# Macaron hybrid layer: another order and other engines for the opening stage's modulation sums and weight splits

## The chip, the cores and the metric

The kernel runs on one core of one Trainium2 chip. The metric is the device time of one execution in microseconds. Engines are named as the profile names them: PE is TensorE (its weight loads are PEld), DVE is VectorE, ACT is ScalarE, POOL is GpSimd, SP is SyncE, which issues the DMAs here. `L89` is line 89 of the kernel before.

## What is computed

One layer over 512 tokens of width 1024: modulation from a condition vector, a gated feed-forward, a mixer (chunked mLSTM and forgetting attention), and a second feed-forward. The change touches the beginning alone:

```python
mod = silu(c) @ w_ada + b_ada                       # c: 1 x 1024, w_ada: 1024 x 9216
sh1, sc1, g1, ... = split(mod, 9)
u = rms_norm(x, ffn1_norm_g) * (1 + sc1) + sh1      # 512 x 1024
a, b = split(u @ ffn1_w_in, 2)                      # ffn1_w_in: 1024 x 5632
x = x + 0.5 * g1 * ((silu(a) * b) @ ffn1_w_out)
```

## The kernel before

Every float32 matmul is made of three in a rounded format: each operand is split into a high part and a remainder, and `uh*wh`, `uh*wl` and `ul*wh` are added up in PSUM. For weights, `split` (L81) makes the high part `wh` on ACT (L88) and the remainder `wl` by a subtraction (L89), on DVE unless another engine is given.

The opening stage is `start` (L397). `x` is loaded and normalised, and then the first 3 of the 22 column pairs of `ffn1_w_in` are multiplied (six PSUM banks, `NJ0` = 3) while the modulation is still being made. A *block* is 128 of the 1024 channels of `u`. For each of the eight blocks k the stage does this:

- `mod(k)` (L432): the shift and scale of the block's 128 channels need `silu(c)` times 1024 x 128 columns of `w_ada`, twice. Four DMAs bring them as eight pieces of 128x256; DVE makes two running sums that take turns (`acc[i % 2]`): two products (L442), six multiply-adds, called *links* here (L444), and an addition of the two (L445). Block 0 is summed on PE instead (`mod0`, L423).
- `load(k)` (L449): the block's feed-forward weights, 128x768, into `raw`, of which there are three buffers.
- `prep(k)` (L452): two one-column matmuls add the sum up over the partitions (L454); two small steps make shift and scale from it (on DVE, L458 and L459; for block 0 on ACT, L461 and L462); four transposes on PE bring the block's `x` (L422); `split` makes `wh` and, on POOL, `wl`; `u_from` (L239) makes `uh` and `uf` on ACT and their difference `ul` (L248), on POOL for block 0, on DVE for the others.
- 18 matmuls on PE (L490). The first three blocks take all six `uh*wh` first, then the six `uh*wl`, then the six `ul*wh`; the others go bank by bank. `prep(k + 1)` is issued behind the seventh.

The order on each engine comes from a scheduler in the framework, by the program's order and a cost estimate; `issue_after` puts an instruction behind another one on the same engine. Each engine runs its instructions in order, and SP issues its DMAs in order too, so that a load that waits for a free buffer holds up those behind it.

Behind the stage `ffn_in` (L333) goes on with the other 19 column pairs, with weights split by `w_stat` (L92), and `ada_row` (L273) makes further rows of the modulation on DVE from 128x1024 loads.

Of the kernel before, what the change touches and what calls it, by code (L numbers as in the profile page):

```python
# [46 lines left out]
class Layer:  # L47
    def __init__(self, tc, es, A, out, dbg=None):
        self.tc, self.nc, self.es, self.A, self.out = tc, tc.nc, es, A, out
        self.dbg = dbg or {}  # L50
# [188 lines left out]
    def u_from(self, ps, k, c0, w, G, sh, pool, start=False):  # L239
# [8 lines left out]
        (nc.gpsimd if (k == 0 if start else k % 2) else nc.vector).tensor_tensor(  # L248
# [148 lines left out]
    def start(self, st, tp):  # L397
# [25 lines left out]
        def mod0():  # L423

            for v in range(2):
                r = st.tile([P, NK, P], F32, name=self.nm("ar"), tag="ar", bufs=15)
                nc.sync.dma_start(r, A["w_ada"][0][:, v * D:v * D + P].rearrange("(i p) n -> p i n", p=P))
                turn(0, (v,))
                turn(1, (v,))
                for i in range(NK):  # L430
                    nc.tensor.matmul(cb[:, 128 * (v + 1):128 * (v + 2)], r[:, i, :], self.ccol[:, i:i + 1].to_broadcast([P, P]), start=i == 0, stop=i == NK - 1)
        def mod(k):  # L432
            acc = [st.tile([P, 2, P], F32, name=self.nm("ac"), tag="ac", bufs=6) for _ in range(2)]
            for q in range(2):
                r = st.tile([P, 4, 2, P], F32, name=self.nm("ar"), tag="ar", bufs=15)
                for v in range(2):
                    nc.sync.dma_start(r[:, :, v, :], A["w_ada"][0][q * 512:(q + 1) * 512, v * D + k * P:v * D + (k + 1) * P]
                                      .rearrange("(i p) n -> p i n", p=P))
                for i in range(4):
                    a, cc = acc[i % 2], self.ccol[:, 4 * q + i:4 * q + i + 1]  # L440
                    if q == 0 and i < 2:
                        nc.vector.tensor_scalar(a, r[:, i], cc, None, op0=MUL)  # L442
                    else:
                        nc.vector.scalar_tensor_tensor(a, r[:, i], cc, a, op0=MUL, op1=ADD)  # L444
# [7 lines left out]
        def prep(k):  # L452
# [3 lines left out]
            wr = raws.pop(k)  # L456
            if k:
                nc.vector.tensor_tensor(m[:, 0:1], cb[:, 2 * k:2 * k + 1], self.colC[:, 16 + k:17 + k], op=ADD)  # L458
                nc.vector.tensor_scalar(m[:, 1:2], cb[:, 2 * k + 1:2 * k + 2], self.colC[:, 8 + k:9 + k], self.colC[:, 24 + k:25 + k], op0=MUL, op1=ADD)  # L459
            else:  # L460
                nc.scalar.activation(m[:, 0:1], cb[:, 128:129], AF.Identity, bias=self.colC[:, 16:17])  # L461
                nc.scalar.activation(m[:, 1:2], cb[:, 256:257], AF.Identity, scale=self.colC[:, 8:9], bias=self.colC[:, 24:25])  # L462
# [612 lines left out]
```

## Time and profile before

| what | us |
|---|---|
| median of three runs | 1375.53 (1375.0 to 1376.16) |
| the profiled execution's own time | 1374.87 |
| its span in the trace | 1372.9 |
| PE busy in the span | 1344.6 |
| DVE busy | 800.8 |
| ACT busy | 554.1 |
| POOL busy | 130.5 |

The trace is that of one execution. Its times count from the span's start. A matmul's duration in the trace overlaps the next one's, so the rate is read from the distance of their starts. Where an engine idles, the row of the timeline names what ended the wait; for a wait on several things that is the last of them as far as the profile can tell, and where the engine named had long been done it was another, often a DMA.

### The profile page before, as it was taken

The numbers are of one execution on the slowest core, as the hardware profiler recorded it, in microseconds if no ns is written. First come the engines' busy times: TensorE is split into PE (matmuls) and PEld (weight loads), VectorE is DVE, ScalarE is ACT, GpSimd is POOL, SyncE is SP. The second block draws the span as 40 slices with busy tenths as digits, with TensorE's granted clock in tenths as the row PEclk, the third lists the DMA queues.
The fourth block names the chain that finished last, engine by engine and source line by source line (L and its number), as shares of the span: only waits on it lengthen the run. The fifth ranks groups of instructions, "written<-read, shape, count | busy, mean of one in ns | idle before, by whom it ended". The sixth has DMA issues, their size and how long they took to land.

```text
span 1372.9 us, 17542 instructions
## 1 busy us (share of the span) xinstructions
PE 1344.6 (98%) x6570; PEld 1126.7 (82%) x6570; DVE 800.8 (58%) x1440; ACT 554.1 (40%) x939; POOL 130.5 (10%) x151
## 2 busy tenths in 40 slices
PE   6999999999999999999999999899999999999998
PEld 5788887887888888888888878788898888888887
DVE  7865666656467776876585876456473333332232
ACT  4442333323237655556565675333262322322120
POOL 4200000000011100313130311002010000000000
PEclk9999999999999999999999999999999999999999
DMA  9766556665534434344343342364323333333330
GB/s 288 206 203 182 181 182 203 210 214 187 184 82 111 121 96 139 118 112 132 88 140 85 112 139 77 117 198 138 107 71 114 92 95 105 92 93 104 102 123 31
DMA packets 217001, 184.42 MB, mean 134 GB/s; under 512 B 10898, under 2 KB 182578, under 8 KB 216916
## 3 DMA queue, kind: packets, MB, share of 16 engines
q1 hardware_dynamic: 216436, 183.22, 44.2%
q8 instruction: 52, 0.85, 0.2%
q14 instruction: 33, 0.27, 0.1%
q0 software_dynamic: 416, 0.06, 0.0%
q10 hardware_dynamic: 64, 0.02, 0.0%
HBM read 172.71 MB, written 10.56 MB: 133 GB/s over the span
## 4 chain that ended last, share of the span: by engine, by line
PE 87%; DVE 7%; ACT 2%; issue 1%; SPq 1%; DMA 1%; POOL 0%; ACTq 0%; DVEq 0%; POOLq 0%
PE g L108 23%; PE g L106 23%; PE g L107 23%; PE t L106 4%; PE t L107 4%; PE t L108 4%; PE t L820 2%; DVE wl L89 1%; PE t L790 1%; PE t L761 1%; PE t L762 1%; DMA ar<-in_w_ada_dram 1%; DVE ac L444 1%; SPq L78 1%; ACT wh L88 1%
## 5 line engine op out<-in xcount | busy, mean ns | idle before, releaser
L89 DVE TENSOR_TENSOR wl<-raw,wh 128x1024 fp32r<-128x1024 f32 x214 | 276.1, 1292 | 277.7 <-ACT wh L88 254.2
L88 ACT ACTIVATE wh<-raw 128x1024 fp32r<-128x1024 f32 (+1 forms) x221 | 231.6, 1053 | 503.4 <-PE g L107 160.3
L108 PE MATMUL g<-uh,wl 128*128 128x512 f32 (+2 forms) x984 | 369.6, 376 | 1.8 <-DVE wl L89 1.8
L106 PE MATMUL g<-uh,wh 128*128 128x512 f32 (+2 forms) x984 | 370.6, 377 | 0.0
L107 PE MATMUL g<-ul,wh 128*128 128x512 f32 (+2 forms) x984 | 369.7, 376 | 0.0
L108 PEld LDWEIGHTS g<-uh,wl 128*128 128x128 f32 (+1 forms) x984 | 184.6, 188 | 36.3 <-DVE wl L89 2.7
L106 PEld LDWEIGHTS g<-uh,wh 128*128 128x128 f32 (+1 forms) x984 | 184.8, 188 | 34.0 <-issue 0.6
L107 PEld LDWEIGHTS g<-ul,wh 128*128 128x128 f32 (+1 forms) x984 | 184.8, 188 | 33.3
L106 PE MATMUL g<-wh,uh 128*128 128x512 f32 (+1 forms) x320 | 111.8, 350 | 0.0
L108 PE MATMUL g<-wh,ul 128*128 128x512 f32 (+1 forms) x320 | 111.1, 347 | 0.0
L107 PE MATMUL g<-wl,uh 128*128 128x512 f32 (+1 forms) x320 | 111.0, 347 | 0.0
L325 DVE TENSOR_TENSOR sl<-g,sl 128x512 f32<-128x512 f32 (+1 forms) x45 | 30.0, 667 | 85.7 <-PE g L108 85.5
L284 DVE SCALAR_TENSOR_TENSOR acc<-raw,ccol,acc 128x1024 f32<-128x1024 f32 x49 | 62.9, 1283 | 15.7 <-DMA raw<-in_w_ada_dram 15.2
L106 PE MATMUL g<-wh,hh 128*128 128x512 f32 x176 | 69.2, 393 | 0.0
L108 PE MATMUL g<-wh,hl 128*128 128x512 f32 x176 | 69.1, 393 | 0.0
L106 PE MATMUL t<-wh,hh 128*128 128x512 f32 x176 | 69.0, 392 | 0.0
L107 PE MATMUL g<-wl,hh 128*128 128x512 f32 x176 | 69.0, 392 | 0.0
L107 PE MATMUL t<-wl,hh 128*128 128x512 f32 x176 | 69.0, 392 | 0.0
L108 PE MATMUL t<-wh,hl 128*128 128x512 f32 x176 | 69.0, 392 | 0.0
L106 PEld LDWEIGHTS g<-wh,uh 128*128 128x128 f32 x320 | 60.5, 189 | 7.8 <-DVE tk L674 0.5
L108 PEld LDWEIGHTS g<-wh,ul 128*128 128x128 f32 x320 | 60.5, 189 | 7.8
L107 PEld LDWEIGHTS g<-wl,uh 128*128 128x128 f32 x320 | 60.5, 189 | 7.4
(264 smaller groups left out, 1921.6 us busy)
## 6 DMA issues: line engine op xcount, KB each, us to landing
raw<-in_ffn_w_in_dram SPq DMA_DIRECT2D x82, 512.0 KB, 3.8
raw<-in_w_ada_dram SPq DMA_DIRECT2D x56, 512.0 KB, 3.4
raw<-in_w_mix_dram SPq DMA_DIRECT2D x48, 512.0 KB, 4.0
raw<-in_ffn_w_out_dram SPq DMA_DIRECT2D x44, 512.0 KB, 3.9
raw<-in_w_mix_dram SPq DMA_DIRECT2D x32, 256.0 KB, 3.0
ar<-in_w_ada_dram SPq DMA_DIRECT2D x28, 256.0 KB, 6.0
g_d<-tg SPq DMA_DIRECT2D x16, 256.0 KB, 3.3
A<-A_d SPq DMA_DIRECT2D x16, 256.0 KB, 3.5
```

Source lines behind the costliest of these rows:

```text
L78: self.nc.sync.dma_start(dst(t), src)
L88: nc.scalar.activation(hi, src, AF.Copy)
L89: (eng or nc.vector).tensor_tensor(lo, src, hi, op=SUB)
L106: mm(ps, lh, rh, start=start, stop=False)
L107: mm(ps, lh, rl, start=False, stop=False)
L108: self.last_mm = mm(ps, ll, rh, start=False, stop=stop)
L284: nc.vector.scalar_tensor_tensor(acc, r, self.ccol[:, k:k + 1], acc, op0=MUL, op1=ADD)
L325: nc.vector.tensor_tensor(s[:, :w], ps_b[:, c0:c1], s[:, :w], op=MUL)
L444: nc.vector.scalar_tensor_tensor(a, r[:, i], cc, a, op0=MUL, op1=ADD)
L761: nc.tensor.matmul(ps[:, :w], q[:, s], k[:, :w], start=True, stop=False)
L762: nc.tensor.matmul(ps[:, :w], q[:, s], kl[:, :w], start=False, stop=True)
L820: nc.tensor.matmul(po[:, q0:], vt[pr][:, kb, i % 2, :], Px[:, o:o + T - q0], start=n == 1, stop=n == 8)
```

## The change

In the opening stage:

- The sum of a block is one chain on DVE: one product and seven links, each on the result of the one before. Blocks 2 and 3, and blocks 4 and 5, are summed in pairs, so that one chain handles 128x512 pieces for two blocks. The loads are cut to match (rows of 1 KB for pairs).
- `wl` is made on DVE for blocks 1 to 7 and on POOL for block 0 alone; block 0's `ul` moves from POOL to DVE.
- Shift and scale are made on ACT for every block.
- `split` for block k + 1 is traced ahead of `prep(k + 1)`, and `mod(k + 2)` behind the former `ul` and `wl`. Loads have their own buffers, eight for `w_ada`, and go ahead of the sums: `fetch`.
- Behind the stage, the first splits and the first product of `ada_row` are put behind the last `uf` and `ul`.

```diff
@@ split
-            nc.scalar.activation(hi, src, AF.Copy)
-        (eng or nc.vector).tensor_tensor(lo, src, hi, op=SUB)
+            with self.tc.issue_after(self.last_uf.ins) if self.lo_after else nullcontext():
+                nc.scalar.activation(hi, src, AF.Copy)
+        with self.tc.issue_after(self.lo_after) if self.lo_after else nullcontext():
+            self.last_lo = (eng or nc.vector).tensor_tensor(lo, src, hi, op=SUB)
@@ u_from
-        (nc.gpsimd if (k == 0 if start else k % 2) else nc.vector).tensor_tensor(
+        self.last_ul = (nc.gpsimd if not start and k % 2 else nc.vector).tensor_tensor(
@@ ada_row
-                nc.vector.tensor_scalar(acc, r, self.ccol[:, 0:1], None, op0=MUL)
+                with self.tc.issue_after(self.last_ul.ins):
+                    nc.vector.tensor_scalar(acc, r, self.ccol[:, 0:1], None, op0=MUL)
@@ start
+        def ada_load(k, n):
+            w = n * P
+            rows = 8 // n
+            ars[k] = []
+            for q in range(n):
+                r = new_ar().rearrange("p (i v c) -> p i v c", v=2, c=w)
+                step = 4 if k == 0 else rows
+                for v in range(2):
+                    for i0 in range(0, rows, step):
+                        r0 = (q * rows + i0) * P
+                        nc.sync.dma_start(r[:, i0:i0 + step, v, :], w_ada[r0:r0 + step * P, v * D + k * P:v * D + k * P + w]
+                                          .rearrange("(i p) n -> p i n", p=P))
+                ars[k].append(r)
...
         def mod(k):
-            acc = [st.tile([P, 2, P], F32, name=self.nm("ac"), tag="ac", bufs=6) for _ in range(2)]
...
-            nc.vector.tensor_tensor(acc[0], acc[0], acc[1], op=ADD)
-            accs[k] = acc[0]
+            tiles = ars.pop(k)
+            n = len(tiles)
+            acc = st.tile([P, 2, n * P], F32, name=self.nm("ac"), tag=f"ac{n}", bufs=4 - n)
+            for i in range(NK):
+                r, cc = tiles[i * n // NK][:, i % (NK // n)], self.ccol[:, i:i + 1]
+                if i:
+                    nc.vector.scalar_tensor_tensor(acc, r, cc, acc, op0=MUL, op1=ADD)
+                else:
+                    nc.vector.tensor_scalar(acc, r, cc, None, op0=MUL)
+            for j in range(n):
+                accs[k + j] = acc[:, :, j * P:(j + 1) * P]
@@ prep
-                nc.vector.tensor_tensor(m[:, 0:1], cb[:, 2 * k:2 * k + 1], self.colC[:, 16 + k:17 + k], op=ADD)
...
+            nc.scalar.activation(m[:, 0:1], c[0], AF.Identity, bias=self.colC[:, 16 + k:17 + k])
+            nc.scalar.activation(m[:, 1:2], c[1], AF.Identity, scale=self.colC[:, 8 + k:9 + k], bias=self.colC[:, 24 + k:25 + k])
...
-                wh, wl = self.split(wr, sh, nc.gpsimd)
+        groups = {0: 1, 1: 1, 2: 2, 4: 2, 6: 1, 7: 1}
+        def fetch(k):
+            ada_load(k, groups[k])
+            for j in range(groups[k]):
+                load(k + j)
@@ loop over the blocks
                 if n == 6 and k + 1 < NK:
+                    ul_ins = self.last_ul.ins
+                    with self.tc.issue_after(self.last_uf.ins):
+                        w = self.split(raws.pop(k + 1), sh)
+                    lo_ins = self.last_lo.ins
                     with self.tc.issue_after(self.last_uf.ins), self.tc.issue_after(mm.ins):
-                        nxt = prep(k + 1)
+                        prep(k + 1)
+                    nxt = w
+                    if k + 2 == NK - 1:
+                        ul_ins = self.last_ul.ins
+                    if k + 2 in groups:
+                        with self.tc.issue_after(ul_ins), self.tc.issue_after(lo_ins):
+                            mod(k + 2)
```

The names below are the program's with running numbers: `ac` a running sum, `ar` its w_ada piece, `raw`, `wh` and `wl` a block's weights, `g_190` to `t_195` the six PSUM banks, `uh_174` and `ul_182` block 0's, the next numbers the next blocks'.

PE in block 0, before: behind the six `uh*wh` and the first `uh*wl` come the one-column matmuls for block 1 (L454) and two transposes.

```order
L490 MATMUL t_195<-uh_174,wh_327 128x512
L490 MATMUL g_190<-uh_174,wl_328 128x512
L454 MATMUL t_196<-one,ac_298 128x1 x2
L422 MATMUL t_273<-ident,xn_237 128x128
L422 MATMUL t_273<-ident,xn_241 128x128
L490 MATMUL g_191<-uh_174,wl_328 128x512
L490 MATMUL g_192<-uh_174,wl_328 128x512
L490 MATMUL g_193<-uh_174,wl_328 128x512
L490 MATMUL t_194<-uh_174,wl_328 128x512
L490 MATMUL t_195<-uh_174,wl_328 128x512
L490 MATMUL g_190<-ul_182,wh_327 128x512
L490 MATMUL g_191<-ul_182,wh_327 128x512
```

The same place now:

```order
L428 MATMUL t_279<-ident,xn_241 128x128
L504 MATMUL g_191<-uh_174,wl_324 128x512
L504 MATMUL g_192<-uh_174,wl_324 128x512
L504 MATMUL g_193<-uh_174,wl_324 128x512
L504 MATMUL t_194<-uh_174,wl_324 128x512
L504 MATMUL t_195<-uh_174,wl_324 128x512
L504 MATMUL g_190<-ul_182,wh_323 128x512
L470 MATMUL t_196<-one,ac_305 128x1 x2
L504 MATMUL g_191<-ul_182,wh_323 128x512
L504 MATMUL g_192<-ul_182,wh_323 128x512
L504 MATMUL g_193<-ul_182,wh_323 128x512
L504 MATMUL t_194<-ul_182,wh_323 128x512
```

The one-column matmuls (L470) stand behind all six `uh*wl` and the first `ul*wh`; five matmuls of block 0 follow them, where eleven did.

DVE from block 1's `ul` on, before: the sum of block 3 (`ac_384`, `ac_385`), with shift and scale of block 2 (L458, L459) and its `ul` in between.

```order
L445 TENSOR_TENSOR ac_331<-ac_331,ac_332 128x256
L442 TENSOR_SCALAR ac_384<-ar_386,ccol 128x256
L442 TENSOR_SCALAR ac_385<-ar_386,ccol 128x256
L444 SCALAR_TENSOR_TENSOR ac_384<-ar_386,ccol,ac_384 128x256
L444 SCALAR_TENSOR_TENSOR ac_385<-ar_386,ccol,ac_385 128x256
L458 TENSOR_TENSOR m_413<-t_196,colC 128x1
L459 TENSOR_SCALAR m_413<-t_196,colC 128x1
L444 SCALAR_TENSOR_TENSOR ac_384<-ar_393,ccol,ac_384 128x256
L444 SCALAR_TENSOR_TENSOR ac_385<-ar_393,ccol,ac_385 128x256
L444 SCALAR_TENSOR_TENSOR ac_384<-ar_393,ccol,ac_384 128x256
L444 SCALAR_TENSOR_TENSOR ac_385<-ar_393,ccol,ac_385 128x256
L248 TENSOR_TENSOR ul_184<-uf_425,uh_176 128x512
```

The same place now, from block 1's remainder on:

```order
L92 TENSOR_TENSOR wl_359<-raw_302,wh_358 128x768
L459 SCALAR_TENSOR_TENSOR ac_305<-ar_299,ccol,ac_305 128x256
L461 TENSOR_SCALAR ac_373<-ar_327,ccol 128x512
L459 SCALAR_TENSOR_TENSOR ac_373<-ar_327,ccol,ac_373 128x512 x3
L251 TENSOR_TENSOR ul_183<-uf_369,uh_175 128x512
L459 SCALAR_TENSOR_TENSOR ac_373<-ar_330,ccol,ac_373 128x512 x2
L92 TENSOR_TENSOR wl_401<-raw_333,wh_400 128x768
L459 SCALAR_TENSOR_TENSOR ac_373<-ar_330,ccol,ac_373 128x512 x2
L251 TENSOR_TENSOR ul_184<-uf_414,uh_176 128x512
```

Two remainders (`wl_359` of block 1, `wl_401` of block 2) stand among the links; `ac_373` is the one chain for blocks 2 and 3, and block 2's `ul` follows it.

DVE at the end of the stage, before: the last links of block 7's sum and block 6's shift and scale, and the next stage's first remainders (L89) ahead of block 7's `ul`.

```order
L444 SCALAR_TENSOR_TENSOR ac_609<-ar_617,ccol,ac_609 128x256
L444 SCALAR_TENSOR_TENSOR ac_608<-ar_617,ccol,ac_608 128x256
L444 SCALAR_TENSOR_TENSOR ac_609<-ar_617,ccol,ac_609 128x256
L458 TENSOR_TENSOR m_637<-t_196,colC 128x1
L459 TENSOR_SCALAR m_637<-t_196,colC 128x1
L445 TENSOR_TENSOR ac_608<-ac_608,ac_609 128x256
L248 TENSOR_TENSOR ul_188<-uf_649,uh_180 128x512
L458 TENSOR_TENSOR m_673<-t_196,colC 128x1
L459 TENSOR_SCALAR m_673<-t_196,colC 128x1
L89 TENSOR_TENSOR wl_790<-raw_787,wh_789 128x1024
L89 TENSOR_TENSOR wl_820<-raw_817,wh_819 128x1024
L248 TENSOR_TENSOR ul_189<-uf_685,uh_181 128x512
```

The same place now:

```order
L251 TENSOR_TENSOR ul_188<-uf_588,uh_180 128x512
L461 TENSOR_SCALAR ac_592<-ar_480,ccol 128x256
L92 TENSOR_TENSOR wl_620<-raw_483,wh_619 128x768
L459 SCALAR_TENSOR_TENSOR ac_592<-ar_480,ccol,ac_592 128x256 x7
L192 COPY colA<-t_666 128x112
L251 TENSOR_TENSOR ul_189<-uf_633,uh_181 128x512
L286 TENSOR_SCALAR acc_800<-raw_802,ccol 128x1024
L92 TENSOR_TENSOR wl_738<-raw_735,wh_737 128x1024
```

All of block 7's sum (`ac_592`) stands behind block 6's `ul`, its links behind block 7's remainder as well; the next stage's first product (`acc_800`) and remainder stand behind block 7's `ul`.

## Rows read from the trace of the kernel before

**Rows 1.** The page: span; busy time, share and instructions of each engine.
```profile
span 1372.9 us, 17542 instructions
PE 1344.6 (98%) x6570; PEld 1126.7 (82%) x6570; DVE 800.8 (58%) x1440; ACT 554.1 (40%) x939; POOL 130.5 (10%) x151
```

**Rows 2.** Stretches: us; busy PE, PEld, DVE, ACT, POOL; granted clock; DMA share; GB/s.
```profile
17.49:66.22 48.73, 42.07 (x198) 33.51 (x199) 44.16 (x88) 19.92 (x28) 15.23 (x8) 0.96 0.87 239
20.00:23.00 3.00, 0.00 (x0) 0.00 (x0) 2.97 (x4) 0.39 (x1) 1.95 (x1) 1.00 1.17 311
23.40:26.70 3.30, 3.30 (x12) 2.82 (x12) 3.20 (x11) 1.88 (x3) 0.00 (x0) 0.50 1.21 297
```

**Rows 3.** Timeline of PE: start, duration, instruction, count, [idle before <-releaser].
```profile
17.49 1.19 PE L490 MATMUL g<-uh,wh 128*128 128x512 f32 x4 [1.19 <-ACT uh L243]
23.21 0.91 PE L454 MATMUL t<-one,ac 128*128 128x1 f32 x4 [3.84 <-DVE ac L445]
24.31 1.63 PE L490 MATMUL g<-uh,wl 128*128 128x512 f32 x3
...
28.07 1.09 PE L490 MATMUL g<-uh,wh 128*128 128x512 f32 x4
...
33.05 1.07 PE L490 MATMUL g<-uh,wh 128*128 128x512 f32 x4
...
43.33 0.39 PE L490 MATMUL g<-uh,wh 128*128 128x512 f32 x1
...
56.52 0.50 PE L490 MATMUL g<-uh,wh 128*128 128x512 f32 x1 [0.82 <-ACT uh L243]
...
61.64 0.39 PE L490 MATMUL g<-uh,wh 128*128 128x512 f32 x1
...
66.22 0.26 PE L187 MATMUL t<-ident,rowsA 112*128 112x112 f32 x1
```

**Rows 4.** Timelines of DVE and, the third row, of POOL in the opening stage.
```profile
16.70 1.05 DVE L442 TENSOR_SCALAR ac<-ar,ccol 128x256 f32<-128x256 f32 x2 [1.25 <-ACT m L462]
...
26.42 0.69 DVE L248 TENSOR_TENSOR ul<-uf,uh 128x512 fp32r<-128x512 f32 x1
...
27.08 2.06 POOL L89 TENSOR_TENSOR wl<-raw,wh 128x768 fp32r<-128x768 f32 x1 [4.66 <-ACT wh L88]
...
27.35 2.20 DVE L442 TENSOR_SCALAR ac<-ar,ccol 128x256 f32<-128x256 f32 x2
...
36.30 1.66 DVE L444 SCALAR_TENSOR_TENSOR ac<-ar,ccol,ac 128x256 f32<-128x256 f32 x4
...
49.76 0.61 DVE L442 TENSOR_SCALAR ac<-ar,ccol 128x256 f32<-128x256 f32 x2
```

**Rows 5.** Timeline of DVE: a 128x512 product, a 128x768 remainder, two dependent links.
```profile
13.98 0.88 DVE L234 TENSOR_SCALAR xn<-x,rq 128x512 f32<-128x512 f32 x2
...
422.64 0.96 DVE L89 TENSOR_TENSOR wl<-rawg,wh 128x768 fp32r<-128x768 f32 x1 [1.95 <-ACT wh L88]
...
424.10 1.54 DVE L549 SCALAR_TENSOR_TENSOR cy<-cz,colA,cy 128x512 f32<-128x512 f32 x2
```

**Rows 6.** Timelines of ACT in blocks 0 and 1 and, last, of PE.
```profile
16.12 0.26 ACT L461 ACTIVATE m<-t,colC 128x1 f32<-128x1 f32 x1 [0.81 <-PE t L431]
16.29 0.34 ACT L462 ACTIVATE m<-t,colC 128x1 f32<-128x1 f32 x1
16.66 0.78 ACT L243 ACTIVATE uh<-t,m 128x512 fp32r<-128x512 f32 x1
17.34 0.77 ACT L245 ACTIVATE uf<-t,m 128x512 f32<-128x512 f32 x1
19.55 0.84 ACT L88 ACTIVATE wh<-raw 128x768 fp32r<-128x768 f32 x1 [1.43 <-DMA raw<-in_ffn_w_in_dram]
...
29.68 0.50 PE L454 MATMUL t<-one,ac 128*128 128x1 f32 x4
```

**Rows 7.** The page's DMA issues: queue, operation, count, KB each, us to landing.
```profile
ar<-in_w_ada_dram SPq DMA_DIRECT2D x28, 256.0 KB, 6.0
```

More of the change, by code (lines that the diff above doesn't have):

```diff
@@ L6 @@
-from contextlib import ExitStack
+from contextlib import ExitStack, nullcontext
 import concourse.bass as bass
@@ L59, in __init__ @@
         self.dp = pool("scr", bufs=1, space=DRAM)
+        self.lo_after = None
         self.n = 0
@@ L338, in ffn_in @@
             self.ffn_h(pa, pb, j, 0, T, hp, tp)
+            self.lo_after = None
             if extra:
@@ L415, in start @@
         cb = self.tbank()
-        accs = {}
-        bt = {}
+        bt, accs, raws, ars = {}, {}, {}, {}
+        w_ada = A["w_ada"][0]
+        new_ar = lambda: st.tile([P, 2048], F32, name=self.nm("ar"), tag="ar", bufs=8)
         def turn(k, tbs):
@@ L422, in turn @@
                 nc.tensor.transpose(bt[k][:, tb * P:(tb + 1) * P], xn[tb][k // 4][:, k % 4 * P:(k % 4 + 1) * P], self.ident)
+        def ada_load(k, n):
[11 more added lines that the diff above has]
+                ars[k].append(r)
         def mod0():
+            r = ars.pop(0)[0]
             for v in range(2):
-                r = st.tile([P, NK, P], F32, name=self.nm("ar"), tag="ar", bufs=15)
-                nc.sync.dma_start(r, A["w_ada"][0][:, v * D:v * D + P].rearrange("(i p) n -> p i n", p=P))
                 turn(0, (v,))
@@ L430, in mod0 @@
                 for i in range(NK):
-                    nc.tensor.matmul(cb[:, 128 * (v + 1):128 * (v + 2)], r[:, i, :], self.ccol[:, i:i + 1].to_broadcast([P, P]), start=i == 0, stop=i == NK - 1)
+                    nc.tensor.matmul(cb[:, 128 * (v + 1):128 * (v + 2)], r[:, i, v, :], self.ccol[:, i:i + 1].to_broadcast([P, P]),
+                                     start=i == 0, stop=i == NK - 1)
         def mod(k):
-            acc = [st.tile([P, 2, P], F32, name=self.nm("ac"), tag="ac", bufs=6) for _ in range(2)]
[L434 to L444, printed above, removed]
-            nc.vector.tensor_tensor(acc[0], acc[0], acc[1], op=ADD)
-            accs[k] = acc[0]
+            tiles = ars.pop(k)
[9 more added lines that the diff above has]
+                accs[k + j] = acc[:, :, j * P:(j + 1) * P]
         sh = [P, 2, NJ0 * P]
-        raws = {}
         def load(k):
@@ L455, in prep @@
             m = sp.tile([P, 2], F32, name=self.nm("m"), tag="m", bufs=4)
-            wr = raws.pop(k)
-            if k:
-                nc.vector.tensor_tensor(m[:, 0:1], cb[:, 2 * k:2 * k + 1], self.colC[:, 16 + k:17 + k], op=ADD)
[L459 to L462, printed above, removed]
+            c = (cb[:, 2 * k:2 * k + 1], cb[:, 2 * k + 1:2 * k + 2]) if k else (cb[:, 128:129], cb[:, 256:257])
+            nc.scalar.activation(m[:, 0:1], c[0], AF.Identity, bias=self.colC[:, 16 + k:17 + k])
+            nc.scalar.activation(m[:, 1:2], c[1], AF.Identity, scale=self.colC[:, 8 + k:9 + k], bias=self.colC[:, 24 + k:25 + k])
             turn(k, range(NT) if k > 1 else (2, 3))
-            if k:
-                wh, wl = self.split(wr, sh, nc.gpsimd)
             self.u_from(bt[k], k, 0, T, m[:, 1:2], m[:, 0:1], tp, True)
-            if not k:
-                wh, wl = self.split(wr, sh, nc.gpsimd, True)
-            return wh, wl
         xn = self.xnorm(0, st) + self.xnorm(1, st)
@@ L473, in start @@
             nc.tensor.transpose(cb[:, 128:256], self.ident, self.ident)
+        groups = {0: 1, 1: 1, 2: 2, 4: 2, 6: 1, 7: 1}
[3 more added lines that the diff above has]
+                load(k + j)
+        fetch(0)
         mod0()
-        load(0)
+        fetch(1)
         mod(1)
-        load(1)
-        nxt = prep(0)
+        prep(0)
+        nxt = self.split(raws.pop(0), sh, nc.gpsimd, True)
+        fetch(2)
         for k in range(NK):
             wh, wl = nxt
-            if k + 2 < NK:
-                mod(k + 2)
-                load(k + 2)
+            ahead = {0: 4, 2: 6, 3: 7}.get(k)
+            if ahead:
+                fetch(ahead)
             uh, ul = self.uh[k], self.ul[k]
```

1 line of the change is left out of this document (added).

## The prediction

> **What bounds the kernel now.** I read the page first: TensorE (PE) is busy 1344.6 of 1372.9 us [rows 1], so time can only be won where PE stands still or runs slowly. The change touches the opening stage alone, so the next view is the table by stretches: from the first block's first matmul (17.49) to the first one after the stage (66.22) are 48.73 us, in which PE is busy 42.07 and the granted clock is 0.96 [rows 2]. Then PE's timeline of that stretch: a block that nothing holds up (block 1, 28.07 to 33.05) takes 4.98 us with its 18 matmuls, 4 transposes and two one-column sums [rows 3]. Eight of those are 39.8 us, so **at most 8.9 us, 0.65%, are to be had**. The losses lie in block 0 (17.49 to 28.07, with 3.84 us of idling until VectorE's first modulation sum and three matmuls in 1.63 us right after it) and from block 4 on (block 4 starts at 43.33, block 6 at 56.52, 13.2 us for two blocks) [rows 3]. Third, VectorE: it waits for POOL. Two 128x256 products take 0.61 us at 49.76, and 2.20 us at 27.35, beside POOL's subtraction that began at 27.08 [rows 4]: 1.59 us lost, and so in five of the blocks (8 us), more in block 1. So the opening hangs on VectorE's queue.
>
> **The change part by part.** Loads by VectorE, first.
> - POOL's subtractions go, but for block 0's: the 1.59 us a block come back. The remainder costs VectorE 0.96 us (128x768 row at 422.64 [rows 5]), 0.88 where an independent instruction follows and overlaps its end; seven are 6.2 us; block 0's `ul` also moves there, 0.69 [rows 4].
> - The sums. Before, two chains take turns: four links take 1.66, a spacing of 0.395 for a duration of 0.475 [rows 4]. One chain makes every link wait for the one before. That price is in the rows: two dependent 128x512 links take 1.54, so 0.785 each for a duration of 0.75 [rows 5], 0.04 after the end of the former. For 128x256 I therefore take 0.515. A single block costs 0.35 + 7 x 0.515 = 3.95 us, a pair 0.48 (a 128x512 product, [rows 5]) + 7 x 0.785 = 5.98. Three singles and two pairs: 23.8 us, where the old form needs about 0.61 + 6 x 0.395 and an addition of about 0.35, 3.3 a block, 23 for seven. The sums get no cheaper.
> - Shift and scale on ScalarE: 0.54 us from the first to the start of `uh` (16.12 to 16.66 [rows 6]). They add nothing to VectorE's queue and don't stand behind its links any more.
>
> Page against rows: the Trainium skill (VectorE: DVE Perf Modes, The DRAIN you can't avoid) says that a semaphore after each instruction costs nothing extra, since the next waits for the pipe to empty anyway; by it a single chain would cost what two do. The rows differ: independent links overlap, dependent ones don't, and I go by the rows.
>
> So VectorE's load falls by some 5 us. But the *order* decides, and I walk it. From the end of a sum to the next block's first matmul are 0.05 (PE wakes) + 0.51 (one-column matmuls, 29.68) + 0.03 + 0.54 (shift, scale) + 0.78 (`uh`) + 0.05 = **1.96 us** [rows 6].
> 1. Up to 17.49 nothing changes; block 0's w_ada comes as four DMAs instead of two, with the same bytes.
> 2. Block 1's sum now needs all of its w_ada. Its first half has landed at 16.70 [rows 4], the weights behind it at 19.55 [rows 6]; by bytes (524 and 393 KB) the second half is there at 18.3. Product and five links to 21.3, `ul` of block 0 to 21.9, link, remainder, link: **23.55**, where the old sum gave 23.21 [rows 3]. PE has by then done all it may of block 0 (its 13th matmul waits for `ul` from 20.7 to 21.9, which this later wait covers). Block 1 starts at 23.55 + 1.96 = 25.5, not at 28.07: the eleven matmuls that stood behind the sum now stand ahead of it. Gain 2.55 us.
> 3. Blocks 2 and 3 share a chain, and block 2 can't start before the sum of both is done. In VectorE's order stand product, three links, `ul`, two links, a remainder, two links: 0.48 + 7 x 0.785 + 0.61 + 0.88, less what overlaps, 7.1 us: **30.7**; block 2 starts at 32.6, against 33.05. PE has been done with block 1 at 30.1. Gain left: 0.4. The loads hold this up little: at 311 GB/s [rows 2] from 19.55 the pair's 2.1 MB are in at 26.3 and block 2's weights at 27.6, and `wh` (0.84) is ready at 28.5, for a remainder due at 28.3.
> 4. Block 4: from block 2's start VectorE has `ul`, the remainder of block 3 (it waits for `wh`, 1.4 after the start), product, two links, `ul`, link, remainder, four links: 9.6 us. Sum at 42.2, block 4 at 44.2, against 43.33: loss 0.85. PE has finished block 3 at 42.2.
> 5. Blocks 5 and 6 then follow at PE's pace, just under 4.98 each [rows 3], since block 6's sum (block 4's start + 7.6) is there as PE comes to it (+ 7.8): block 6 at 54.05, against 56.52. Gain 2.5.
> 6. Block 7's sum stands behind block 6's `ul` (54.6 to 55.3) and, but for its product, behind a remainder: 0.35 + 0.88 + 7 x 0.515, that is **59.9**; block 7 starts at 61.8, against 61.64. PE ends block 6 at 58.6 and waits 3.2 us. The whole gain of step 5 is gone.
> 7. Block 7 takes 4.2, PE goes on at 66.0, against 66.22: **-0.2 us**.
>
> Costed at nothing: behind the stage the first ada product now stands ahead of the first remainder of the next stage on VectorE; that is ready about 2 us after `ul`, while PE has 13 matmuls (3.0 us) before it asks. On SP each weight load now waits for VectorE's remainder three blocks back instead of POOL's, and the next w_ada loads queue behind it: block 7's stand behind a load that waits for block 3's remainder (35), land some 6 us after their issue [rows 7], and are asked for at 55. Without those 14 us of cover every microsecond of lateness would count in full. The profiled execution took 1374.87 for a span of 1372.9; less 0.2 it is 1374.7. The median of the runs, 1375.53, lies 0.66 above the profiled one, so I forecast **1375.3**.
>
> **The rivals.**
> *Slower: PE's clock falls in the new pauses.* Before, after PE's 3.84 us of idling, the granted clock was 0.50 from 23.4 to 26.7 [rows 2]: 1.2 instead of 2.4 GHz, matmuls 0.43 apart instead of 0.23 [rows 3], so 3.3 us for 1.65 us of work. The new walk has pauses before block 1 (2.6 us, cut by a matmul), before block 2 (2.5) and before block 7 (3.2, with 0.5 of sums in it). Each is shorter than the 3.84 that was seen to do it, and I can't tell from what length it does. A fall after the first costs 0.6 (the sum of the pair hides the rest), after the second 1.05, after the third 1.6. One: 1376 to 1377; the last two together 1378.0; all three 1378.6, slower by the bound below. The Trainium skill's page TensorE: Matmul & The Clock Gate (What's actually happening) calls the slow rate the default, which activity lifts; the row agrees, and says nothing on pauses of this size.
> *Faster: the freed VectorE reaches PE.* If the sums of blocks 2, 4 and 7 came before PE asks, the waits of 2.5, 2.0 and 3.2 would go: 1367.6, and 1371.5 with half of it. For it speaks that VectorE loses 5 us of load; against it, the fixed order, where each sum has its predecessor's work ahead of it.
> *Cheaper links.* If a dependent link costs what an independent one does (0.12 less, 21 such links on the walk), it is 2.5 us: 1372.8. The 1.54 for two [rows 5] speaks against it. This is also what the Trainium skill's rule (VectorE: DVE Perf Modes, The DRAIN you can't avoid) gives.
> *No effect in VectorE* (POOL's subtraction wasn't what held it): then steps 3 to 6 are as long, since POOL isn't in them; it gives the same time.
>
> **How the numbers follow.** A measurement of this kernel can tell about 0.2%, 2.75 us: faster means below 1372.8, slower above 1378.3. The walk as told 0.50 (1375.3); one or two falls of the clock 0.24 (1376 to 1378); cheaper links 0.08 (1372.8 to 1374); the sums off the path 0.10 (1367.6 to 1372); three falls or a late load besides 0.08 (1378.6). That is faster 0.10, same 0.82, slower 0.08. The range takes in the walk, the cheaper links and two falls: 1372.8 to 1377.9, which leaves 0.18 outside.
>
> **What would show it.** In the changed profile: no 128x256 product over 0.4 us after 18; links 0.51 and 0.78 apart; block 1 starting near 25.5, block 2 near 32.6, block 4 near 44.2, block 6 near 54, block 7 near 61.8; PE idle before blocks 2, 4 and 7 on the one-column matmuls; the next stage at 66.0. I am wrong if block 2 starts before 31 or block 7 before 60 (sums off the path), or if the granted clock shows a second stretch at 0.5 in the stage.

## The result, and the profile of the changed kernel

The changed kernel takes 1378.43 us (median of 14 runs, 1375.39 to 1379.87), the kernel before 1375.63 in runs on the same chips (14 runs, 1374.39 to 1376.53). The ratio is 1.0021, with a 95% interval of 1.0013 to 1.0029: 2.8 us slower, where 1375.3 was forecast and the range ended at 1377.9. The profiled execution took 1378.32 us for a span of 1376.5. These lines of its page stand against [rows 1]:

```profile
span 1376.5 us, 17489 instructions
PE 1347.5 (98%) x6570; PEld 1129.4 (82%) x6570; DVE 791.8 (58%) x1411; ACT 557.1 (40%) x953; POOL 115.6 (8%) x143
```

DVE has 9 us less to do, where the prediction had some 5, and POOL has 15 less. PE has the same 6570 instructions and is busy 2.9 us *longer*. Work on PE that grows without an instruction points to another rate, so the next view is the table by stretches (us; busy PE, PEld, DVE, ACT, POOL; granted clock; DMA share; GB/s), against [rows 2]:

```profile
17.12:23.70 6.58, 3.87 (x16) 2.64 (x17) 5.21 (x11) 1.46 (x2) 0.03 (x1) 1.00 1.09 350
23.70:30.50 6.80, 6.80 (x21) 5.53 (x21) 6.33 (x10) 2.69 (x5) 0.00 (x0) 0.50 1.09 357
30.60:47.50 16.90, 14.09 (x72) 11.60 (x72) 9.39 (x14) 7.61 (x15) 0.00 (x0) 1.00 0.87 251
47.60:51.00 3.40, 3.40 (x14) 2.83 (x14) 3.02 (x6) 0.99 (x4) 0.00 (x0) 0.50 0.23 67
51.10:70.30 19.20, 17.06 (x82) 13.52 (x81) 12.14 (x22) 9.76 (x17) 0.00 (x0) 1.00 0.28 83
```

The kernel before has one stretch of 3.3 us at a granted clock of 0.50 in this stage [rows 2]. The changed one has 10.2 us of it: 6.8 from 23.70, and 3.4 from 47.60. PE's timeline shows where they lie (start, duration, instruction, count, [idle before <-releaser]); L504 are the blocks' matmuls, L470 the one-column ones, L190 is a transposition for the next stage, and L109 is the first matmul behind the stage:

```profile
17.12 1.19 PE L504 MATMUL g<-uh,wh 128*128 128x512 f32 x4 [1.19 <-ACT uh L246]
...
21.93 0.50 PE L504 MATMUL g<-ul,wh 128*128 128x512 f32 x1 [1.55 <-DVE ul L251]
23.59 0.94 PE L470 MATMUL t<-one,ac 128*128 128x1 f32 x4 [1.16 <-DVE ac L459]
24.39 1.63 PE L504 MATMUL g<-ul,wh 128*128 128x512 f32 x3
...
26.67 1.91 PE L504 MATMUL g<-uh,wh 128*128 128x512 f32 x4
...
33.04 0.50 PE L470 MATMUL t<-one,ac 128*128 128x1 f32 x4
34.95 1.23 PE L504 MATMUL g<-uh,wh 128*128 128x512 f32 x4 [1.40 <-ACT uh L246]
...
46.60 0.50 PE L504 MATMUL g<-uh,wh 128*128 128x512 f32 x1 [1.41 <-ACT uh L246]
...
58.35 0.40 PE L504 MATMUL g<-uh,wh 128*128 128x512 f32 x1
...
62.80 0.39 PE L504 MATMUL t<-ul,wh 128*128 128x512 f32 x1
64.23 0.61 PE L470 MATMUL t<-one,ac 128*128 128x1 f32 x4 [1.05 <-DVE ac L459]
65.43 0.32 PE L190 MATMUL t<-ident,rowsA 112*128 112x112 f32 x1 [0.59 <-ACT m L474]
66.24 0.50 PE L504 MATMUL g<-uh,wh 128*128 128x512 f32 x1 [0.49 <-ACT uh L246]
...
70.48 0.39 PE L109 MATMUL g<-uh,wh 128*128 128x512 f32 x1
```

PE stands still for 1.55 and 1.16 us, with one matmul between, and then runs block 0's last five matmuls and most of block 1 at half rate: 24.39 to 26.02 for three. Before the second slow stretch stands a pause of 1.41. From block 0's first matmul to the next stage it is now 53.36 us (17.12 to 70.48), where it was 48.73 [rows 2]. Behind 70.48 the span is no longer than behind 66.22 before (1306.0 against 1306.7), so **the whole loss is made in the opening stage**.

DVE meanwhile does what the walk said, block 1's sum to 0.01 us and the pair's to 0.35 (against [rows 4, 5]):

```profile
18.32 0.35 DVE L461 TENSOR_SCALAR ac<-ar,ccol 128x256 f32<-128x256 f32 x1 [3.06 <-DMA ar<-in_w_ada_dram]
18.71 2.57 DVE L459 SCALAR_TENSOR_TENSOR ac<-ar,ccol,ac 128x256 f32<-128x256 f32 x5
...
23.06 0.48 DVE L459 SCALAR_TENSOR_TENSOR ac<-ar,ccol,ac 128x256 f32<-128x256 f32 x1
...
26.59 0.69 DVE L251 TENSOR_TENSOR ul<-uf,uh 128x512 fp32r<-128x512 f32 x1 [0.30 <-ACT uf L248]
...
29.52 1.53 DVE L459 SCALAR_TENSOR_TENSOR ac<-ar,ccol,ac 128x512 f32<-128x512 f32 x2
...
60.57 3.60 DVE L459 SCALAR_TENSOR_TENSOR ac<-ar,ccol,ac 128x256 f32<-128x256 f32 x7
```

Product at 18.32 where 18.3 was expected, links 0.52 apart, block 1's sum at 23.54 (23.55), the pair's at 31.05 (30.7). The 0.35 are in the main a wait of 0.30 for block 1's `uf`, which came late because PE was late.

### The profile page after: what moved, and what is told of

Its sections match the earlier page's. It is cut to its first block, busy times and chain, and to the rows that moved or that the text cites. A ratio compares the mean times of both kernels' runs of the same rounds, so it can differ in the third digit from the quotient of the medians.

```text
span 1376.5 us, 17489 instructions
## 1 busy us (share of the span) xinstructions
PE 1347.5 (98%) x6570; PEld 1129.4 (82%) x6570; DVE 791.8 (58%) x1411; ACT 557.1 (40%) x953; POOL 115.6 (8%) x143
## 4 chain that ended last, share of the span: by engine, by line
PE 88%; DVE 7%; ACT 3%; issue 1%; SPq 1%; DMA 1%; POOL 0%; DVEq 0%; ACTq 0%; POOLq 0%
PE g L109 23%; PE g L111 23%; PE g L110 23%; PE t L109 4%; PE t L110 4%; PE t L111 4%; PE t L846 2%; PE g L504 1%; DVE wl L92 1%; PE t L816 1%; PE t L787 1%; PE t L788 1%; PE t L504 1%; DMA ar<-in_w_ada_dram 1%; DVE ac L459 0%
## 5 line engine op out<-in xcount | busy, mean ns | idle before, releaser
L92 DVE TENSOR_TENSOR wl<-raw,wh 128x1024 fp32r<-128x1024 f32 (+1 forms) x221 | 281.8, 1276 | 276.3 <-ACT wh L90 258.3
L109 PE MATMUL g<-uh,wh 128*128 128x512 f32 (+2 forms) x984 | 370.5, 377 | 0.3 <-ACT wh L90 0.3
L109 PEld LDWEIGHTS g<-uh,wh 128*128 128x128 f32 (+1 forms) x984 | 184.8, 188 | 34.2 <-ACT wh L90 0.9
L109 PE MATMUL g<-wh,uh 128*128 128x512 f32 (+1 forms) x320 | 111.9, 350 | 0.0
L109 PE MATMUL g<-wh,hh 128*128 128x512 f32 x176 | 69.2, 393 | 0.0
L109 PE MATMUL t<-wh,hh 128*128 128x512 f32 x176 | 69.0, 392 | 0.0
L109 PEld LDWEIGHTS g<-wh,uh 128*128 128x128 f32 x320 | 60.5, 189 | 7.8 <-DVE tk L700 0.5
```

What stands on the lines that cost most here:

```text
L92: self.last_lo = (eng or nc.vector).tensor_tensor(lo, src, hi, op=SUB)
L109: mm(ps, lh, rh, start=start, stop=False)
```

## The experiments

**Theory A:** the order of the sums is worth about nothing, as the walk has it, and the 2.8 us are the granted clock, which falls in PE's new pauses. **Rival B:** a part of the new order costs the time by itself, whatever the clock: the pairs, the place of block 7's sum, the remainders on DVE, shift and scale on ACT. **Rival C:** the clock falls for another reason than the pauses.

To tell A from C the pauses are filled with work that does nothing: matmuls with weights of zero that add to an open bank.

**Block 0's pauses filled** (`e1_fill_block0`).

```diff
+        zero = st.tile([P, P], F32R, name="zero")
+        nc.gpsimd.memset(zero.bitcast(F32), 0.0)
+        def warm(n, mm):
+            for _ in range(n):
+                with self.tc.issue_after(mm.ins):
+                    mm = nc.tensor.matmul(acc_ps[5], zero, self.uh[0], start=False, stop=False)
+            return mm
...
+                if k == 0 and n in (11, 12):
+                    mm6 = warm({11: 6, 12: 5}[n], mm)
```

> The changed kernel with eleven more 512-column products on TensorE in block 0's two pauses: six ahead of block 0's first product on ul, five behind it and ahead of block 1's one-column products. Their weights are zeros and they add to a bank that is already open, so they add work and nothing else; one remainder on VectorE stands one link earlier. Theory A (the granted clock falls because TensorE stands still twice between 20.4 and 23.6, and the 0.50 stretch from 23.7 to 30.5 is what makes it late): the stretch at 0.50 there is gone, block 1 starts near 25.5 instead of 26.67 and ends near 30.2, block 2 starts near 32.9 instead of 34.95, the kernel takes 1375.5 to 1376.8 (a fall near 47 may stay). Rival B (the order of the sums costs it, whatever the clock): the stretch goes and the kernel stays at 1378 or more. Rival C (the clock falls for a reason other than the pauses): the stretch at 0.50 stays, and 1378.4 or more.

Measured: 1377.96 us (11 runs), ratio 1.0019 (1.0010 to 1.0027). Its table by stretches:

```profile
17.50:45.10 27.60, 24.22 (x115) 18.91 (x116) 20.72 (x32) 11.37 (x21) 0.04 (x1) 1.00 1.08 327
45.20:48.50 3.30, 3.30 (x13) 2.78 (x12) 2.99 (x6) 1.37 (x4) 0.00 (x0) 0.50 0.05 13
48.70:65.60 16.90, 14.75 (x73) 11.69 (x71) 9.52 (x20) 7.47 (x13) 0.00 (x0) 1.00 0.31 90
65.70:69.00 3.30, 3.30 (x10) 2.52 (x9) 2.63 (x4) 2.34 (x4) 0.00 (x0) 0.50 0.48 124
```

The edit is shown in part; its other lines hold transposes, one-column matmuls and links of blocks 1 and 2 at given places, and on DVE one remainder stands a link earlier. The stretch of 6.8 us is gone, so C falls for this one. The blocks moved as A says (PE's timeline):

```profile
25.93 1.19 PE L513 MATMUL g<-uh,wh 128*128 128x512 f32 x4
...
33.10 1.20 PE L513 MATMUL g<-uh,wh 128*128 128x512 f32 x4 [1.40 <-ACT uh L246]
...
44.72 0.50 PE L513 MATMUL g<-uh,wh 128*128 128x512 f32 x1 [1.41 <-ACT uh L246]
...
64.33 0.50 PE L513 MATMUL g<-uh,wh 128*128 128x512 f32 x1 [0.49 <-ACT uh L246]
...
70.16 0.40 PE L109 MATMUL g<-uh,wh 128*128 128x512 f32 x1
```

Block 1 starts at 25.93 and block 2 at 33.10, 1.85 us earlier than in the changed kernel, block 4 at 44.72, 1.9 earlier. But the clock falls again behind the pause before block 4 and behind those before block 7, and the gain is given back: the next stage starts at 70.16. The total missed A's number (1376.8 at most) and came to within 0.04 us of B's (1378), for a reason that is A's. It leaves the question open whether the order alone is innocent.

**All pauses filled** (`f1_fill_all`): the same, with six such matmuls also ahead of blocks 2, 4 and 7, and four ahead of block 7's one-column ones.

> The changed kernel with products on zero weights in all of TensorE's pauses of the opening: eleven in block 0 (as in the run before), six behind the one-column products of block 2, six behind those of block 4, four ahead and six behind those of block 7. The sums, loads and copies stay. Theory A (the 3 us are the granted clock, the order itself is worth about nothing): the stretches at 0.50 inside the opening are gone; block 2 near 33, block 4 near 44.7, block 7 near 62.5 to 63, the total 1375.0 to 1376.0, no more than 1.001 of before. Rival B (the order costs it): 1377.5 or more with the clock at 1.00. Also possible: the clock falls in spite of the added products; then no verdict on the order from this run.

Measured: 1375.96 us (12 runs), ratio 1.0001 (0.9993 to 1.0010). In the table by stretches the stage is one at full clock:

```profile
18.11:68.20 50.09, 49.60 (x237) 39.27 (x238) 36.95 (x61) 24.10 (x43) 0.04 (x1) 1.00 0.73 220
```

PE's timeline has the starts of blocks 1, 2, 4 and 7 and of the next stage:

```profile
26.24 1.20 PE L514 MATMUL g<-uh,wh 128*128 128x512 f32 x4
...
33.42 1.20 PE L514 MATMUL g<-uh,wh 128*128 128x512 f32 x4
...
45.06 0.50 PE L514 MATMUL g<-uh,wh 128*128 128x512 f32 x1
...
62.88 0.50 PE L514 MATMUL g<-uh,wh 128*128 128x512 f32 x1
...
67.13 0.47 PE L109 MATMUL g<-uh,wh 128*128 128x512 f32 x1
```

Same sums, same loads, same copies, and 2.5 us less than the changed kernel: **A holds for the forecast: what it missed is the granted clock.** Of the order by itself the run says less. It comes out level with the kernel before (-1.0 to +1.4 us by the interval), but that kernel has a slow stretch of 3.3 us in its own stage [rows 2]: the stage takes 49.02 us here at full clock, and it took 48.73 with that stretch in it. So the order gains nothing against that, and at equal clock it seems to lose (table by clock, below); the kernel before was not run with its own pause filled, which would settle it. It is the cleanest of the runs for the walk, too. From block 0's first matmul (18.11 here, 17.49 in the walk) the walk put blocks 1, 2, 4, 7 and the next stage at 8.0, 15.1, 26.7, 44.3 and 48.5 us; here they come at 8.1, 15.3, 27.0, 44.8 and 49.0.

**The parts of the order, one at a time.** Four runs undo one part each.

Block 7's sum freed (`e3_block7_early`):

```diff
-                    if k + 2 == NK - 1:
-                        ul_ins = self.last_ul.ins
```

> The changed kernel without the line that holds block 7's sum until block 6's ul is done, so this sum may start some us earlier. Theory A: the stretches at 0.50 at 23.7 and near 47 stay, blocks 1 to 6 start where they do now (block 2 at 34.95, block 4 at 46.6); only the last wait, 1.05 and 0.49 us ahead of block 7, goes: 1376.5 to 1378.4. Rival B (the place of block 7's sum is what costs the 2.8 us): back to 1375.6 or below.

Measured: 1376.07 us (11 runs, 1372.48 to 1377.24), ratio 0.9998 (0.9989 to 1.0007): 2.4 us less than the changed kernel, more than A had given it and less than B. Block 7's product and six of its seven links now run ahead of block 6's `ul` instead of behind it; on DVE's timeline (two of these eight links are block 6's):

```profile
53.94 3.75 DVE L459 SCALAR_TENSOR_TENSOR ac<-ar,ccol,ac 128x256 f32<-128x256 f32 x8
```

On PE's, its one-column matmuls wait for nothing:

```profile
59.46 0.50 PE L470 MATMUL t<-one,ac 128*128 128x1 f32 x4
```

By stretches, the clock still falls twice in the stage, and in this execution twice more outside it (first and last row):

```profile
12.20:15.50 3.30, 3.30 (x18) 3.30 (x17) 2.84 (x13) 1.53 (x3) 0.03 (x1) 0.50 1.16 315
25.90:29.10 3.20, 3.20 (x9) 2.42 (x10) 3.17 (x5) 1.25 (x2) 0.00 (x0) 0.50 1.09 355
29.30:46.20 16.90, 14.09 (x73) 11.65 (x72) 10.20 (x16) 7.40 (x15) 0.00 (x0) 1.00 0.99 283
46.30:49.60 3.30, 3.30 (x14) 2.78 (x12) 3.15 (x6) 1.06 (x3) 0.00 (x0) 0.50 0.16 48
869.00:875.60 6.60, 5.82 (x14) 4.57 (x15) 4.97 (x9) 4.27 (x8) 0.00 (x0) 0.50 0.62 196
```

The other nine traces have one slow stretch near 870, half as long, and none at 12. The stage is 47.71 us long here (18.86 to 66.57), shorter than the 48.73 of the kernel before in spite of its two falls.

So these two lines are where the gain of the rest of the order is lost, as step 6 said. Freeing the sum is worth 2.4 us here, and 2.9 between the two filled kernels (1375.96 above and 1373.05 below); filling the pauses is worth 2.5 with the late sum and 3.0 with the early one. Each is about as large as the 2.8 us by which the changed kernel trails, and either alone brings it level with the kernel before. The cost of the late sum was in the forecast; that of the clock was not.

No pairs (`e2_no_pairs`; each block has a chain of its own and loads of 512-byte rows):

```diff
-        groups = {0: 1, 1: 1, 2: 2, 4: 2, 6: 1, 7: 1}
+        groups = {k: 1 for k in range(NK)}
...
+        fetch(3)
...
-            ahead = {0: 4, 2: 6, 3: 7}.get(k)
+            ahead = {0: 4, 1: 5, 2: 6, 3: 7}.get(k)
```

> The changed kernel with no pairs: every block sums its own 256 columns in one chain of eight, at about 0.515 a link (4.1 us a block, plus ul 0.69 and wl 0.95 a block); the loads come as 512-byte rows a block. Block 2's sum then ends near 29.4 instead of 31.05, and block 7's near 59 to 60 as before. Theory A: the two pauses of block 0 are the same, so the clock falls at 23.7 here too and TensorE ends block 1 near 33, not waiting for block 2's sum; the kernel comes to 1376 to 1378, by how many stretches at 0.50 follow. Rival B (pairs make TensorE wait for a sum twice as long): faster by the two waits of 1.4 us, 1375 to 1376, whatever the clock does.

Measured: 1377.4 us (11 runs), ratio 1.0012 (1.0004 to 1.0021), within A's range and outside B's. The pauses of block 0 are there as in the changed kernel, and so is a slow stretch of 6.7 us, which begins in the second of them; the waits of 1.4 ahead of blocks 2 and 4 are gone, with waits of 0.6 ahead of blocks 3 and 5 in their place, and a late fall stays, behind the waits for block 7 (stretches):

```profile
22.70:29.40 6.70, 5.64 (x15) 4.66 (x16) 6.26 (x13) 2.69 (x5) 0.00 (x0) 0.50 1.17 310
29.50:63.50 34.00, 30.76 (x152) 23.65 (x150) 24.79 (x50) 14.43 (x28) 0.00 (x0) 1.00 0.74 201
63.60:66.90 3.30, 3.06 (x7) 2.48 (x8) 2.47 (x4) 2.75 (x4) 0.00 (x0) 0.50 0.06 6
```

The remainders back on POOL (`e4_wl_on_pool`):

```diff
-                        w = self.split(raws.pop(k + 1), sh)
+                        w = self.split(raws.pop(k + 1), sh, nc.gpsimd)
```

> The changed kernel with the weights' remainders of blocks 1 to 7 back on POOL, everything else as changed. By the rows of before such a remainder takes 2.2 us on POOL and the links on VectorE that meet it wait for it. Theory A: block 1's and the pairs' sums end where they do or up to 1 us a block later, block 0's pauses grow, the clock falls as often as now: 1378 to 1380. Rival B (the seven remainders of 0.95 us that VectorE took over are what delays the sums): sums end earlier by about 1 us a block and the kernel takes 1375 to 1376.5.

Measured: 1382.37 us (5 runs), ratio 1.0049 (1.0035 to 1.0063), worse than either had it. Five links take 4.15 us instead of 2.57, because POOL's subtraction falls into them, and PE waits 4.62 for the first sum. The timeline of DVE:

```profile
19.04 4.15 DVE L459 SCALAR_TENSOR_TENSOR ac<-ar,ccol,ac 128x256 f32<-128x256 f32 x5
```

of POOL:

```profile
20.58 1.80 POOL L92 TENSOR_TENSOR wl<-raw,wh 128x768 fp32r<-128x768 f32 x1 [3.00 <-ACT wh L90]
```

and of PE:

```profile
24.75 0.59 PE L470 MATMUL t<-one,ac 128*128 128x1 f32 x2 [4.62 <-DVE ac L459]
```

The five runs' mean clock is 0.994 to 0.995, as in nearly all of the changed kernel's, so it is not the clock. This part of the change is a gain of 3.9 us in this order (1382.37 to 1378.43), and no rival.

Shift and scale back on DVE (`f5_mod_on_dve`):

```diff
-            nc.scalar.activation(m[:, 0:1], c[0], AF.Identity, bias=self.colC[:, 16 + k:17 + k])
-            nc.scalar.activation(m[:, 1:2], c[1], AF.Identity, scale=self.colC[:, 8 + k:9 + k], bias=self.colC[:, 24 + k:25 + k])
+            if k:
+                nc.vector.tensor_tensor(m[:, 0:1], c[0], self.colC[:, 16 + k:17 + k], op=ADD)
+                nc.vector.tensor_scalar(m[:, 1:2], c[1], self.colC[:, 8 + k:9 + k], self.colC[:, 24 + k:25 + k], op0=MUL, op1=ADD)
...
```

> The changed kernel with shift and scale of blocks 1 to 7 back on VectorE. Either theory: VectorE now waits inside its queue for the one-column products between two links, by the rows of before some tenths of a us a block, so the pairs' sums end 0.3 to 0.8 us later a block and the kernel takes 1378.4 to 1380; if ScalarE is the slower place (0.53 us from the first of the two to uh), 1377.5 to 1378.4.

Measured: 1378.3 us (9 runs), ratio 1.002 (1.0011 to 1.0030): no different from the changed kernel, and in the range given for ScalarE as the slower place. DVE now waits 0.71 us for PE between the pair's product and its links, and block 2 follows its one-column matmuls 0.1 us sooner (1.81 against 1.91); neither shows in the total.

**What beats both kernels.** Theory A says which: the order without its late sum, and without the pauses. Two runs tried it.

`f2_fill_early7` is the all-filled kernel without the two lines on block 7 (and without the matmuls that filled that pause):

> The same with block 7's sum free to start early (the line removed that holds it behind block 6's ul), and products on zero weights only in the pauses that are left: eleven in block 0, six ahead of block 2, six ahead of block 4. The runs of the kernel with block 7's sum early took 1372.6 us where the mean clock was 0.997 and 1376.7 where it was 0.994. Theory A: all runs go to 1372 to 1373.2, faster than before by 0.15 to 0.25%. Rival B (those fast runs are something else than the clock): 1375 to 1376.5 as without the added products.

Measured: 1373.05 us (11 runs, 1371.96 to 1373.54), ratio 0.9980 (0.9971 to 0.9988): the median lies in A's range, single runs up to 0.3 us above it. Against `e3_block7_early` only the 23 added matmuls and the places of a few instructions beside them differ: work was added to PE, and the median went down by 3.0 us. (The two were run on two chips, on which the kernel before took 1375.33 and 1375.52.) The profiled executions don't show all of that in the stage: they lie 3.8 us apart, of which 1.0 is the stage (47.71 and 46.70), 1.45 lies ahead of block 0 and 1.3 behind the stage, where the kernel without the products had its further falls. The filled kernel's stage is one stretch at full clock, 46.70 us long to the next stage's first matmul (17.41 to 64.11):

```profile
17.41:65.00 47.59, 47.08 (x226) 37.29 (x227) 37.42 (x62) 24.04 (x43) 0.04 (x1) 1.00 0.77 235
```

`f4_early7_no_pairs` undoes pairs and late sum, and adds nothing:

> No pairs and block 7's sum free to start early, no added products. Theory A: as the kernel without pairs, less the wait of 1.15 + 0.59 + 0.49 us ahead of block 7: 1377.4 - 2.2 = 1375.2 where two stretches at 0.50 stay, 1373 where one does; spread by mean clock. If pairs were what costs (B), under 1373 in the median whatever the clock.

Measured: 1373.49 us (11 runs, 1372.20 to 1374.94), ratio 0.9983 (0.9975 to 0.9992). That is near A's 1373 for one fall, and not under 1373, as B had it. It has one fall in the stage, behind block 0's pauses, and waits of 0.6 us ahead of blocks 3 and 5 (stretches):

```profile
24.50:27.80 3.30, 3.30 (x9) 2.54 (x8) 3.19 (x7) 2.49 (x5) 0.00 (x0) 0.50 1.17 308
27.90:65.00 37.10, 35.72 (x176) 28.06 (x175) 30.10 (x59) 19.44 (x36) 0.00 (x0) 1.00 0.77 212
```

Without pairs and with block 0's pauses filled was not tried.

**The same kernel, by its clock.** Every run comes with the mean granted clock of its whole span, and that gives the comparison that no edit can: runs of one kernel against each other. Mean time in us, and in brackets the number of runs (of the kernel before, the 33 beside the second group of experiments; `e4_wl_on_pool` and `f5_mod_on_dve` left out):

| kernel | 0.994 | 0.995 | 0.996 | 0.997 | 0.998 | 0.999 |
|---|---|---|---|---|---|---|
| before | | 1376.5 (6) | 1375.8 (15) | 1374.9 (12) | | |
| changed | 1379.7 (2) | 1378.4 (10) | 1377.4 (1) | 1375.4 (1) | | |
| block 0's pauses filled | 1379.9 (2) | 1379.2 (2) | 1377.9 (5) | 1376.4 (2) | | |
| no pairs | | 1377.7 (9) | 1376.6 (1) | 1375.2 (1) | | |
| all pauses filled | | 1378.7 (1) | | 1376.4 (5) | 1375.3 (2) | 1374.6 (4) |
| block 7 early | 1376.7 (6) | 1376.1 (1) | 1374.0 (1) | 1372.6 (3) | | |
| block 7 early, filled | | | | 1373.2 (7) | 1372.4 (4) | |
| block 7 early, no pairs | | | 1374.1 (6) | 1372.4 (4) | 1372.6 (1) | |

Read along a row, a thousandth of clock is 0.6 to 2.1 us but for one single run. The changed kernel had one run in 14 at 0.997, the kernel before 12 in 33, and that one run took 1375.39. Read down a column, the changed order is behind the kernel before: 1.9 us at 0.995 (10 runs and 6), 1.6 at 0.996 and half a us at 0.997 (one run each), and with all its pauses filled 1.5 at 0.997 (five). The three with block 7 early are 1.7 to 2.5 ahead there. So of the 2.8 us the higher share of slow clock is one part and the order, with its late sum, the other; the filled kernel comes level with the kernel before because its clock is higher than that one's. The mean clock is that of the whole span, and each of the ten traces has a slow stretch near 870 as well, so the columns don't say where the clock fell. In the filled kernel's runs at 0.997 it fell somewhere more often than in the one profiled, which had no fall in the stage; where, no trace shows.

## Why the prediction was wrong, point by point

- *What bounds the kernel* (the opening hangs on DVE's queue): right for the sums, and incomplete. PE's rate is a second bound, and it hangs on PE's own pauses.
- *Step 1*: nothing changed up to block 0 (17.12 against 17.49).
- *Step 2*: the sum came at 23.54, as said. Block 1 then started at 26.67 and not 25.5. The one-column matmuls and the five products behind them ran at a granted clock of 0.50. In the all-filled run the step holds (8.1 us after block 0's start, 8.0 said).
- *Step 3*: the sum was there at 31.05 (30.7), but PE was not: it ended block 1 at 33.0, not 30.1, since the slow stretch went on to 30.5. **This is the step that failed.** Steps 2 and 3 take PE at full clock across the new pauses, so that the sum has a fall at nothing; the rival has it at 0.6 us, since "the sum of the pair hides the rest". That price was taken from a stretch of 3.3 us [rows 2]; here it was 6.8, and block 2 was 2.5 us later (17.8 after block 0's start, 15.3 in the all-filled run). The price is low even for 3.3 us: half of them, 1.65, are lost, and by the walk's own times the sum hides 0.6 of that (30.1 to 30.7), which leaves 1.05. In `e3_block7_early`, whose first fall in the stage was of 3.2 us, block 2 came 3.05 behind the end of the sum (30.80 to 33.85), where the walk has 1.96.
- *Step 4*: from block 2's start to block 4's it is 11.65 us, as said (11.6); the 2.4 us that block 4 is late are step 3's.
- *Step 5*: block 6 started 11.75 after block 4 and not 9.85, because of the second fall: in the all-filled run it is 10.13 (45.06 to 55.19).
- *Step 6*: right, and confirmed by `e3_block7_early` and `f2_fill_early7`. Block 7's sum took 3.60 us behind block 6's `ul` and ended at 64.17, block 7 followed 2.07 later (1.96 said). The wait is as long as said: from the end of block 6's matmuls (62.80, and 0.23 to where the next could start) to block 7 are 3.2 us, in which PE idles for 1.05, 0.59 and 0.49 and does its one-column matmuls and a transposition. So this wait took up nothing of what the falls had cost, since block 7's sum starts behind block 6's `ul` and came late with it.
- *Step 7*: 70.48 and not 66.0; from block 0's start 53.36 us and not 48.5, of which step 3 is 2.5 to 2.8 and step 5 is 1.9.
- *Costed at nothing*: right for what it lists. The loads, the transition behind the stage and SP's queue show up nowhere; behind the stage the trace is no longer than before. PE's clock, which the walk also had at nothing, is not listed.
- *The rivals.* What came is *PE's clock falls in the new pauses*. Its mechanism was told, and so was the place of the first fall; the second came behind the pause ahead of block 4, which the walk has (42.2 to 44.2) and the rival leaves out. It also came with the sign that the prediction had named, a second stretch at 0.5 in the stage. That the price for three falls, 1378.6, is near what was measured is luck: the trace has two, one of them twice as long as the one they were priced by. Its chance was too small: 0.24 for one or two falls, and a part of 0.08 for three. The reason given against it was that each pause is "shorter than the 3.84 that was seen to do it". One instance that does something gives no lower end: falls came behind pauses of 1.55 and 1.16, and behind single ones of 1.41, 1.31 (`f5_mod_on_dve`) and 1.16 (`e3_block7_early`, ahead of block 1) as well. *Cheaper links* is out (0.52 and 0.78 apart), *the freed VectorE reaches PE* as well (the waits ahead of blocks 2, 4 and 7 came). *No effect in VectorE* is refuted by `e4_wl_on_pool`: POOL's subtraction did hold the links, and would cost 3.9 us.
- On the Trainium skill's rule of the pipe that is emptied after each instruction (VectorE: DVE Perf Modes, The DRAIN you can't avoid), rows decide as the prediction had it: dependent 128x256 links stand 0.52 apart, the kernel before has independent ones 0.395 apart [rows 4].

So the sum of the change stands where the clock does (1375.3 forecast, 1375.96 with the pauses filled, 1375.39 in the changed kernel's one run at 0.997), and the time was missed, because the likeliest case took the clock for granted.

**Open:** why the 1.40 us ahead of block 2 brought no fall in any of these traces while the 1.41 ahead of block 4 did in three; what decides between 3.4 and 6.8 us at the lower clock; and what the kernel before would take with its own pause filled. Runs of the same code spread by 4 us and more, so the order alone does not decide it.

## What to carry to other kernels

When a change moves PE's idle time, list the pauses before and after, and price each new one as a possible fall of the clock, also where it is shorter than any that has been seen to do it; a row of short pauses can cost more than its own length. Compare PE's busy time for the same number of instructions: if it grows, look at the granted clock by stretches before you look for a cause in the order. And where PE bounds a stage, work that does nothing, put into an unavoidable pause, can win time (2.5 us for 33 added matmuls in the changed kernel, by medians, and 3.0 for 23 with block 7's sum early, not all of it in the stage), and an order with fewer pauses gets nearly as far without it (1373.49 against 1373.05).

## What the runs showed of the hardware that was not expected

- A slow stretch can last while PE works without a break: from 23.70 to 30.50 PE was busy 6.80 of 6.80 us, and the granted clock was 0.50 throughout. In the kernel before such a stretch was 3.3 us long [rows 2], after a longer pause (3.84 us [rows 3]). The Trainium skill (TensorE: Matmul & The Clock Gate, What's actually happening) says that activity lifts the lower rate; here it did so late.
- Pauses of 1.4 us, far shorter than the 3.84 of before, can be followed by a fall (46.60 in the changed kernel, 44.72 in the first filled one). The length alone does not decide it: a pause of 3.66 or 3.67 near 870 went with a fall in all ten traces; one of 2.02 ahead of block 0 did in `e3_block7_early`, and one of 2.08 at the same place in the all-filled run did not.
- How often the clock falls is not the same in each run: the changed kernel's mean clock lay between 0.994 and 0.997, and its time between 1379.87 and 1375.39.
- POOL's 128x768 subtraction holds DVE's multiply-adds for nearly all of its 1.80 us: 1.58 more for the five that it met.
